# A streaming encoder layer on one core: token-major values first, 24 projection tiles in pairs by seven half products, the other tiles as fillers

## The chip, the cores and the metric

The kernel runs on one core of a Trainium2 chip. TensorE does the matmuls and transposes, VectorE, ScalarE and GpSimd the elementwise work, and SyncE (SP) issues most of the transfers. The metric is the device time of one execution in microseconds; less is better. In the program's names PE is TensorE, DVE is VectorE, ACT is ScalarE and POOL is GpSimd.

## What is computed

One inference step of one layer for 1024 tokens of a new stream and 16 tokens of each of 8 running streams: 1152 tokens, in 9 tiles of 128. In float32, cut to what matters:

```
h = rms_norm(x, norm_g);  z = h @ w_in + b_in       # (1152, 1024) @ (1024, 6664)
mq, mk, mv, mo, mz, mi, mf, aq, ak, av, az, gm, ga = split(z)
q, k = silu(causal_conv(mq, mk))                     # 4 heads of 128
h_m  = sigmoid(mo) * rms_norm(mlstm_chunks(q, k, mv, mi, mf))
q, k = rms_norm per head of 64 of (aq, ak)           # 8 heads of 64
h_a  = softmax(q @ k / 8 + rel_bias) @ av            # band of 512 + own chunk, cache for the running streams
u_m  = (h_m * silu(mz)) @ w_bm;  u_a = (h_a * silu(az)) @ w_ba
y    = x + (sigmoid(gm) * u_m + sigmoid(ga) * u_a) @ w_out
```

The other outputs are the new mLSTM states, the last rows ahead of the convolution, and the new keys and values.

## The kernel before, in words

Matmuls keep float32 accuracy by splitting both operands: a value is `hi`, its rounding to a shorter format, and `lo`, the rest. `split` lets ScalarE make `hi` and another engine (VectorE unless told otherwise) `lo`, and `mm3` gives three matmuls for one product: hi·hi, hi·lo, lo·hi.

```
def mm3(ps, lhs, rhs, first, last):
    mm(ps, lhs[0], rhs[0], start=first, stop=False)
    mm(ps, lhs[0], rhs[1], start=False, stop=False)
    mm(ps, lhs[1], rhs[0], start=False, stop=last)
```

The normed input stays on chip as `h_hi`, `h_lo`: features on partitions (8 k-tiles of 128), tokens along the columns. A projection tile is 128 output features: `load_nt` brings 128 weights x 8 k in two pieces of 512 columns (`wr`, then `wh` and `wl`), `feature_tile` goes over three chunks of 384 tokens with 8 `mm3` each. So a tile is 72 matmuls of 384 columns. The 36 tiles of `wn` are mq, mk, mo and mz (4 each), az (4), gm and ga (8 each). Token-major products have the tokens on the output's partitions: the values mv with the gates i and f (`mv_half`, 264 and 256 columns, weights `w_hi`, `w_lo`), and q, k, v of a pair of attention heads (`qkv`, 384 columns).

The stages are: prenorm of the 9 token tiles, with the first half of the values in between; `gate_rows`, which turns i and f into the decay rows of the mLSTM (ten small transposes `pg`, and a chain of small operations on VectorE and ScalarE between them); convolutions (`conv_part`: first tap on ScalarE, three on VectorE, then tanh and a product) with the projections mq, mk of the same tile; the second half of the values; then per head h the inputs of head h+1, `gate_unit` (mo and mz) and `mlstm_head(h - 1)`. So projections stand beside memory and output chains in this whole part.

In the attention the order of TensorE's work is written by a planner in the kernel: chains `attend(p, i)` (pair p, token tile i: transposes of q and k, scores `pS`, softmax, transposes `pT`, values `pv`) and `sample(p)` are threads that go on when the planner's clock `line.now` says that what they wait for should be there; between them it puts one `mm3` (three matmuls, counted as 480 ns) of `pair_work` (the q, k, v of the next pair), then of `tile_work` (az, gm, ga), then of `um_work` (w_bm). The tile az of the next pair waits until the old pair's tiles are done. At the end stand w_ba and w_out. A tile framework puts the instructions on the engines' queues and adds the semaphores; on each engine they run in that order. SP's list is one such queue: a DMA that waits for its source holds back those behind it.

## Time and profile before

| what | value |
|---|---|
| time, median of 3 runs | 1078.8 us (1077.47 to 1081.25) |
| span of the profiled execution | 1075.1 us |
| TensorE busy, matmuls | 1055.1 us, 98% |
| TensorE busy, weight loads (beside the matmuls) | 1024.3 us |
| VectorE busy | 658.3 us, 61% |
| ScalarE busy | 421.3 us, 39% |
| GpSimd busy | 241.4 us, 22% |
| DMA | 131.58 MB, mean 122 GB/s |

The busy time of a matmul runs until its modelled end, so that neighbours overlap: 0.33 us busy stand behind a start every 0.17 us. What a matmul takes from TensorE is therefore read from the starts in a timeline. A wait is put down to the semaphore that came last.

### The profile page before, as it was taken

To read this page: it belongs to the slowest core of one execution; us is meant where nothing else is said; L and a number is where in the kernel's file an instruction comes from. 1 tells how busy PE (TensorE), PEld (TensorE's weight loads), DVE (VectorE), ACT (ScalarE), POOL (GpSimd) and SP (SyncE) were. 2 spreads that over 40 slices of the span, in tenths; PEclk is the share of its full clock that TensorE was granted. 3 is DMA by queue.
4 is the path that set the end of the run, shared out by engine and by line. 5 is a ranking of instruction groups with operands and counts; after the bars stand their busy time and mean duration, and the time that the engine had idled before them with its cause. 6 is when DMAs were issued, how large, how long until landed. Compare 5 with 4: busy or idle time off the path is not lost.

```text
span 1075.1 us, 19715 instructions
## 1 busy us (share of the span) xinstructions
PE 1055.1 (98%) x7078; PEld 1024.3 (95%) x7078; DVE 658.3 (61%) x1931; ACT 421.3 (39%) x976; POOL 241.4 (22%) x406
## 2 busy tenths in 40 slices
...
PEclk9999999999999999999999999999999999999999
...
GB/s 241 161 88 61 101 66 53 87 121 101 116 85 127 151 146 167 117 76 111 114 126 99 62 148 137 54 71 141 111 79 84 111 262 243 202 223 106 136 143 67
DMA packets 115664, 131.58 MB, mean 122 GB/s; under 512 B 28197, under 2 KB 91885, under 8 KB 115566
## 3 DMA queue, kind: packets, MB, share of 16 engines
...
q14 instruction: 42, 0.34, 0.1%
...
## 4 chain that ended last, share of the span: by engine, by line
PE 88%; DMA 6%; DVE 3%; ACT 1%; issue 1%; SPq 1%; POOL 0%; DVEq 0%; ACTq 0%
PE pm L114 24%; PE pm L116 24%; PE pm L115 24%; PE pT L570 3%; PE pv L732 3%; DMA v_sc<-vt 1%; PE pS L702 1%; PE pS L703 1%; DMA tm<-tg_sc 1%; PE pv L816 1%; DMA xt<-in_x 1%; DMA sm_sc<-tm 1%; DMA raw<-o_sc 1%; PE mA L495 1%; PE mS L477 1%
## 5 line engine op out<-in xcount | busy, mean ns | idle before, releaser
L114 PE MATMUL pm<-h_hi,wh 128*128 128x384 f32 x1056 | 357.4, 339 | 3.2 <-DVE tm L904 3.1
L116 PE MATMUL pm<-h_hi,wl 128*128 128x384 f32 x1056 | 357.5, 339 | 0.0
L115 PE MATMUL pm<-h_lo,wh 128*128 128x384 f32 x1056 | 356.9, 338 | 0.0
L114 PEld LDWEIGHTS pm<-h_hi,wh 128*128 128x128 f32 x1056 | 198.4, 188 | 8.0 <-DVE tm L904 3.2
L116 PEld LDWEIGHTS pm<-h_hi,wl 128*128 128x128 f32 x1056 | 198.3, 188 | 1.3
L115 PEld LDWEIGHTS pm<-h_lo,wh 128*128 128x128 f32 x1056 | 198.4, 188 | 0.6
L114 PE MATMUL pm<-w_hi,h_hi 128*128 128x384 f32 (+2 forms) x432 | 142.6, 331 | 8.2 <-DVE vt L243 5.4
L116 PE MATMUL pm<-w_hi,h_lo 128*128 128x384 f32 (+2 forms) x432 | 140.0, 325 | 1.2 <-DVE h_lo L100 1.2
L115 PE MATMUL pm<-w_lo,h_hi 128*128 128x384 f32 (+2 forms) x432 | 139.9, 325 | 0.0
L99 ACT ACTIVATE wh<-wr 128x512 fp32r<-128x512 f32 x104 | 65.1, 628 | 170.9 <-PE pm L115 131.8
L100 DVE TENSOR_TENSOR wl<-wr,wh 128x512 fp32r<-128x512 f32 x100 | 77.6, 776 | 68.1 <-ACT wh L99 68.0
L114 PEld LDWEIGHTS pm<-w_hi,h_hi 128*128 128x128 f32 x432 | 82.3, 191 | 13.8 <-DVE vt L243 6.0
L562 ACT ACTIVATE prob<-prob,mx 128x640 f32<-128x640 f32 (+4 forms) x72 | 51.2, 711 | 86.4 <-DVE mx L561 66.5
L116 PEld LDWEIGHTS pm<-w_hi,h_lo 128*128 128x128 f32 x432 | 82.4, 191 | 2.7 <-DVE h_lo L100 1.7
L564 POOL TENSOR_SCALAR prob<-prob,mx 128x640 f32<-128x640 f32 (+4 forms) x72 | 50.7, 704 | 150.2 <-DVE mx L563 83.7
L115 PEld LDWEIGHTS pm<-w_lo,h_hi 128*128 128x128 f32 x432 | 82.5, 191 | 0.1
L114 PE MATMUL pm<-x_hi,wh 128*128 128x384 f32 x192 | 65.1, 339 | 0.0
L116 PE MATMUL pm<-x_hi,wl 128*128 128x384 f32 x192 | 65.0, 339 | 0.0
L115 PE MATMUL pm<-x_lo,wh 128*128 128x384 f32 x192 | 65.0, 338 | 0.0
L559 DVE CUSTOM_DVE_ANT_0 prob<-pS,bias 128x640 f32<-128x640 f32 (+4 forms) x64 | 41.8, 654 | 16.6 <-PE pT L570 8.4
L981 POOL TENSOR_TENSOR sa<-sa 128x384 f32<-128x384 f32 x24 | 27.7, 1163 | 107.2 <-DVE sa L980 107.2
L994 DVE SCALAR_TENSOR_TENSOR xr<-pm,xr 128x384 f32<-128x384 f32 x24 | 13.4, 558 | 62.2 <-PE pm L116 62.2
...
## 6 DMA issues: line engine op xcount, KB each, us to landing
wr<-in_wn SPq DMA_DIRECT2D x72, 256.0 KB, 2.9
...
kr<-in_Kc SPq DMA_DIRECT2D x16, 512.0 KB, 5.2
vr<-in_Vc SPq DMA_DIRECT2D x16, 512.0 KB, 5.2
...
xt<-in_x SPq DMA_DIRECT2D x9, 512.0 KB, 5.3
...
```

The lines of the kernel that those rows point to most:

```text
L99: act.activation(out=hi, in_=raw, func=AF.Copy)
L100: eng.tensor_tensor(out=lo, in0=raw, in1=f(hi), op=ALU.subtract)
L114: mm(ps, lhs[0], rhs[0], start=first, stop=False)
L115: mm(ps, lhs[0], rhs[1], start=False, stop=False)
L116: mm(ps, lhs[1], rhs[0], start=False, stop=last)
L559: dve.tensor_tensor_reduce(out=view, in0=pS, in1=bias, scale=1.0, scalar=-3e38, op0=ALU.add, op1=ALU.max, accum_out=mx[:, 0:1])
L562: act.activation(out=pt[:, :nk], in_=pt[:, :nk], func=AF.Exp, bias=mx[:, 1:2], accum_out=mx[:, 2:3])
L564: pool.tensor_scalar(out=pt[:, :nk], in0=pt[:, :nk], scalar1=mx[:, 3:4], scalar2=1.0, op0=ALU.mult, op1=ALU.mult)
L570: pe.transpose(pT[:, n * P:(n + 1) * P], pt[:, n * P:(n + 1) * P], ident)
L732: mm(pv[:, j * 256:(j + 1) * 256], at("Vst")[:, i + 1 - nb + n, j, :], st[:, n].rearrange("p a q -> p (a q)"), start=n == 0, stop=n == nb - 1)
L981: pool.tensor_tensor(out=sm[:, s], in0=sm[:, s], in1=ta[:, s], op=ALU.add)
L994: dve.scalar_tensor_tensor(out=xr, in0=ps.rearrange("p (i t) -> p i t", i=3), scalar=0.5, in1=xr, op0=ALU.mult, op1=ALU.add)
```

## The change

The whole front part of the program is written in another order, and 24 of the 44 projection tiles are computed in another way.

- The prenorm leaves the input in quarters: k-tiles 0 to 3 and 4 to 7 (`h1`, `h2`), tokens 0 to 575 and 576 to 1151 (`h21` is k 0 to 3 of the second half). For tokens of the second half it also makes four sums and differences of quarters, `S1` to `S4`, each split into hi and lo.
- Then all values, mv and av, token-major, in four passes over the nine tiles with four sets of weights; the results go to `v_sc` in DRAM. `h21` is stored to `h_sc`.
- Then 12 pairs of tiles: aq with ak (with the norm of q and k feature-major, by a matmul with a block of ones, `pN`), mq with mk, mo with mz. A pair is a product of a 2 x 2 block of weight halves with a 2 x 2 block of input quarters; it is computed with seven half products instead of eight (`chunk_of`), 4 k-tiles and 288 columns each, twice for the two chunks of a half. The weight sums come from GpSimd (`sub` in `pair_weights`), the sums of results from VectorE and GpSimd. Outputs go to `qk_sc`, `u_sc`, `g_sc` in DRAM.
- Then `h21` is loaded back, `gate_rows`, `head_inputs` (which now reads `u` from DRAM), and the four mLSTM heads, with two tiles of gm behind each. The tiles, now in four chunks of 288 columns, take `lo` of their weights from GpSimd.
- The attention reads q, k and v from DRAM (`load_q`, `load_kv`); the transposes of q and k and `pair_work` are gone; 8 gate tiles, az and w_bm are what the planner can put between the chains, and it counts 520 ns for three such matmuls. The keys leave the kernel feature-major and are transposed on the host.

```diff
+    h1 = [hp.tile([P, KH, HF], F32R, name=f"h1_{q}") for q in ("hi", "lo")]
+    h2 = [hp.tile([P, KH, T], F32R, name=f"h2_{q}") for q in ("hi", "lo")]
...
+        if n1 < P:
+            n, s = P - n1, slice(c0 + n1 - HF, c1 - HF)
+            x21, x22 = (px[:, :, n1:P] for px in pxs)
+            s1, s2 = (x0.tile([P, KH, P], F32, tag="sx", name="sx", bufs=5)[:, :, 0:n] for _ in range(2))
+            act.activation(out=s1, in_=x22, func=AF.Copy)
+            dve.tensor_tensor(out=s1, in0=x21, in1=s1, op=ALU.add)
+            x11, x12 = (x0.tile([P, KH, P], F32, tag="sx", name="sx", bufs=5)[:, :, 0:n] for _ in range(2))
+            pool.tensor_tensor(out=x11, in0=f(h1[0][:, :, s]), in1=f(h1[1][:, :, s]), op=ALU.add)
+            pool.tensor_tensor(out=x12, in0=f(h2[0][:, :, s]), in1=f(h2[1][:, :, s]), op=ALU.add)
+            pool.tensor_tensor(out=s2, in0=s1, in1=x11, op=ALU.subtract)
+            split(S_hi[0][:, :, s], S_lo[0][:, :, s], s1, pool)
+            split(S_hi[1][:, :, s], S_lo[1][:, :, s], s2, pool)
+            s3 = x0.tile([P, KH, P], F32, tag="sx", name="sx", bufs=5)[:, :, 0:n]
+            dve.tensor_tensor(out=s3, in0=x11, in1=x21, op=ALU.subtract)
+            split(S_hi[2][:, :, s], S_lo[2][:, :, s], s3, pool)
+            pool.tensor_tensor(out=s2, in0=x12, in1=s2, op=ALU.subtract)
+            split(S_hi[3][:, :, s], S_lo[3][:, :, s], s2)
...
+    wts = None
+    for i in range(NT):
+        prenorm(i)
+        if i == 0:
+            wts = value_weights(0, pool)
+        values(0, i, wts)
+    for u in range(1, 4):
+        wts = value_weights(u, dve)
+        for i in range(NT):
+            values(u, i, wts)
+    for q in range(2):
+        sp.dma_start(h_sc[q], f(h21[q]))
...
+    def pair_weights(n1, n2):
+        def load(n, q):
+            t_ = wp.tile([P, KH, P], F32, tag="wr", name="wr", bufs=7)
+            sp.dma_start(t_, a["wn"][n][:, KH * q:KH * q + KH, :])
+            return t_
+        def halves(x):
+            hi = wp.tile([P, KH, P], F32R, tag="wh", name="wh", bufs=8)
+            lo = wp.tile([P, KH, P], F32R, tag="wl", name="wl", bufs=8)
+            split(hi, lo, x)
+            return hi, lo
+        def sub(out, x, y):
+            pool.tensor_tensor(out=out, in0=x, in1=y, op=ALU.subtract)
+        b11, b12, b22, b21 = load(n1, 0), load(n2, 0), load(n2, 1), load(n1, 1)
+        w = {1: halves(b11)}
+        sub(b11, b12, b11)
+        w[5] = halves(b11)
+        t2 = wp.tile([P, KH, P], F32, tag="t2", name="t2", bufs=1)
+        sub(t2, b22, b11)
+        w[6] = halves(t2)
+        w[2] = halves(b21)
+        w[3] = halves(b22)
+        sub(b12, b22, b12)
+        w[7] = halves(b12)
+        sub(b21, b21, t2)
+        w[4] = halves(b21)
+        return w
+    def product(ps, w, x, first):
+        for k in range(KH):
+            for l, r in ((0, 0), (0, 1), (1, 0)):
+                mm(ps, w[l][:, k, :], x[r][:, k, :], start=first and k + l + r == 0, stop=k == KH - 1 and l == 1, skip_group_check=True)
...
+    def chunk_of(w, s, ev):
+        X, W, Z = (pp.tile([P, 512], F32, tag=t_, name=t_)[:, :HC] for t_ in ("pX", "pW", "pZ"))
+        p1, p5, u2, t_ = buf(), buf(), buf(), buf()
+        product(X, w[1], quarter(0, 0, s), True)
+        act.activation(out=p1, in_=X, func=AF.Copy)
+        product(W, w[5], sums(1, s), True)
+        act.activation(out=p5, in_=W, func=AF.Copy)
+        pool.tensor_tensor(out=t_, in0=p1, in1=p5, op=ALU.add)
+        product(Z, w[6], sums(2, s), True)
+        add(dve, u2, Z, p1)
+        yield
+        product(X, w[2], quarter(0, 1, s), False)
+        ev(0, 0, s, X, False)
+        product(W, w[3], sums(4, s), False)
+        add(dve, u2, W, u2)
+        ev(1, 0, s, u2, True)
+        product(Z, w[7], sums(3, s), False)
+        add(dve, t_, Z, t_)
+        ev(1, 1, s, t_, True)
+        yield
+        product(Z, w[4], quarter(1, 1, s), False)
+        add(dve, p1, Z, p1)
+        ev(0, 1, s, p1, True)
+        yield
...
+        def ev(e, half, s, x, own):
+            n = 36 + 4 * e + p
+            z, y, t_ = (x if own else buf()), buf(), buf()
+            c, b = (wp.tile([P, HC], F32R, tag=f"sq{q}", name="sq", bufs=2) for q in range(2))
+            act.activation(out=z, in_=x, func=AF.Identity, bias=bn[:, n:n + 1])
+            act.activation(out=y, in_=z, func=AF.Square)
+            split(c, b, y, pool)
+            pn = pp.tile([P, 512], F32, tag="pN", name="pN")[:, :HC]
+            mm(pn, onesb, c, start=True, stop=False)
+            mm(pn, onesb, b, start=False, stop=True)
+            act.activation(out=y, in_=pn, func=AF.Ln, scale=1.0 / 64, bias=eps)
+            act.activation(out=y, in_=y, func=AF.Exp, scale=-0.5)
+            dve.scalar_tensor_tensor(out=t_, in0=y, scalar=-0.5 / 64, in1=y, op0=ALU.mult, op1=ALU.mult)
+            dve.scalar_tensor_tensor(out=t_, in0=pn, scalar=64 * EPS, in1=t_, op0=ALU.add, op1=ALU.mult)
+            dve.scalar_tensor_tensor(out=y, in0=t_, scalar=1.5, in1=y, op0=ALU.add, op1=ALU.mult)
+            dve.scalar_tensor_tensor(out=z, in0=z, scalar=gqk[:, e:e + 1], in1=y, op0=ALU.mult, op1=ALU.mult)
+            c_ = cols(half, s)
+            sp.dma_start(qk_sc[4 * e + p][:, c_], z)
...
+    jobs = [(36 + p, 40 + p, ev_norm(p)) for p in range(4)]
+    jobs += [(h, 4 + h, ev_plain(h, 4 + h)) for h in range(4)]
+    jobs += [(8 + h, 12 + h, ev_gate(h)) for h in range(4)]
+    last = None
+    for n1, n2, ev in jobs:
+        w = pair_weights(n1, n2)
+        for s in range(2):
+            ch = chunk_of(w, s, ev)
+            next(ch)
+            if last:
+                next(last)
+            next(ch)
+            last = ch
+    next(last)
...
+    h21 = [hq.tile([P, KH, HF], F32R, name=f"h21_{q}") for q in ("hi", "lo")]
+    for q in range(2):
+        sp.dma_start(f(h21[q]), h_sc[q])
...
+    def conv_part(nt, out):
...
-        def ev(c, ps):
-            lo, hi = c * CH, min((c + 1) * CH, TP)
-            act.activation(out=u[:, 3 + lo:3 + hi], in_=ps[:, :hi - lo], func=AF.Identity, bias=bn[:, nt:nt + 1])
-            if hi == TP:
...
-        feature_tile(w, h_rhs, ev)
+        sp.dma_start(u[:, 3:3 + TP], u_sc[nt][:, 0:TP])
+        sp.dma_start(us[:, :, 3:], u_sc[nt][:, TP:T].rearrange("p (b t) -> p b t", b=NB))
...
-    mv_half(0)
     gate_rows()
     prev = head_inputs(0)
-    mv_half(1)
...
-    gate_unit(0)
-    for h in range(1, 4):
-        cur = head_inputs(h)
-        gate_unit(h)
-        mlstm_head(h - 1, *prev)
-        prev = cur
-    mlstm_head(3, *prev)
-    for j in range(3):
-        feature_tile(load_nt(a["wn"][20 + j]), h_rhs, g_evac(j))
+    for h in range(4):
+        nxt = head_inputs(h + 1) if h < 3 else None
+        mlstm_head(h, *prev)
+        prev = nxt
+        for _ in range(2):
+            j = gates.pop(0)
+            feature_tile(load_nt(a["wn"][20 + j], eng=pool), h_rhs, g_evac(j), n=HC)
...
     def attend(p, i):
-        while (p, i) not in made:
+        while p and ("s", p - 1, NPT - 1) not in done:
             yield
-        zt, zd, t_ = made[p, i]
-        yield from until(t_)
+        if i == 0:
+            load_bias(p)
+            load_q(p, 1)
...
-        sX.give(t_)
-        sZ.give(t_)
...
         done.add(("s", p, i))
+        if i == 3 and p < 3:
+            load_q(p + 1, 0)
+            load_kv(p + 1)
...
         while p < 4 or gates:
             if p < 4 and (not p or all((p - 1, i) in done for i in range(6))):
-                w = load_nt(a["wn"][16 + p])
-                ev = silu_evac(16 + p, lambda c: at("za")[:, c * CH:(c + 1) * CH])
-                for c in range(NCH):
+                w = load_nt(a["wn"][16 + p], eng=pool)
+                ev = silu_evac(16 + p, lambda c: za[:, c * HC:(c + 1) * HC])
+                for c in range(4):
...
     def um_work():
...
-            w = load_nt(a["wbm"][j], 4)
-            for c in range(NCH):
+            w = load_nt(a["wbm"][j], 4, eng=pool)
+            for c in range(4):
                 yield from chunk(c, w, h_rhs, um_evac(j), 4)
```

The instructions on TensorE where `gate_rows` starts, in the program before (L114 to L116 are the three matmuls of `mm3`, `pg` the transposes of `gate_rows`):

```order
L115 MATMUL pm<-h_lo,wh 128x384
L254 MATMUL pg<-ident,gscr 36x128
L255 MATMUL pg<-ident,gscr 36x128
L116 MATMUL pm<-h_hi,wl 128x384
...
L114 MATMUL pm<-h_hi,wh 128x384
L274 MATMUL pg<-ident,gscr 1x36
...
L275 MATMUL pg<-ident,gscr 1x36
L116 MATMUL pm<-h_hi,wl 128x384
...
L291 MATMUL pg<-ident,gscr 32x1
L292 MATMUL pg<-ident,gscr 32x1
L116 MATMUL pm<-h_hi,wl 128x384
```

The same place after the change, between the last half product (L322) and the first tile of gm (L123 to L125):

```order
L322 MATMUL pZ<-h_lo,wh 128x288
L322 MATMUL pZ<-h_hi,wl 128x288
L505 MATMUL pg<-ident,G 36x128
L506 MATMUL pg<-ident,G 36x128
L525 MATMUL pg<-ident,gscr 1x36
L526 MATMUL pg<-ident,gscr 1x36
L542 MATMUL pg<-ident,gscr 32x1
L543 MATMUL pg<-ident,gscr 32x1
L573 MATMUL pg<-ident,gscr 128x36 x4
L123 MATMUL pm<-h_hi,wh 128x288
```

Before, 35, 4 and 24 projection matmuls stand between the groups of transposes shown; after, all ten transposes stand in one block with none between.

SP's list at that place after the change (`g_sc<-ring` stores of the last pairs, `u` the input of a convolution, `wr` the weights of the first tile of gm):

```order
L411 DMA g_sc<-ring 128x288
L513 DMA gscr<-in_m 4x8
L592 DMA u<-in_convst 128x8x3
L593 DMA u<-u_sc 128x1024
L594 DMA u<-u_sc 128x8x16
L411 DMA g_sc<-ring 128x288
...
L434 DMA h_hi<-h_sc 128x2304
L434 DMA h_lo<-h_sc 128x2304
...
L570 DMA M_sc<-gscr 36x128
L445 DMA wr<-in_wn 128x512
```

Before, a weight load was ahead of the store of the decay rows there:

```order
L284 DMA out_mp<-gscr 1x4
L106 DMA wr<-in_wn 128x512
L290 DMA dec_sc<-gscr 1x32
...
L305 DMA DEC<-dec_sc 128x64
L106 DMA wr<-in_wn 128x512
L319 DMA M_sc<-gscr 36x128
L420 DMA Mb<-M_sc 128x9x128
```

What moved: `u` is a transfer now and not written by ScalarE, it is issued after a store of the last pair, and the first weights of gm come behind the store of the decay rows.

TensorE where a pair takes over from the one ahead of it in the attention, before (`pX` transposes of q and k, `pS` scores, `pv` values, `pT` transposes of the probabilities):

```order
L115 MATMUL pm<-w_lo,h_hi 128x384
L702 MATMUL pS<-Kst,q_hi 128x128
L703 MATMUL pS<-Kst,q_lo 128x128
L579 MATMUL pX<-ident,zd 128x128 x2
L116 MATMUL pm<-w_hi,h_lo 128x384
L114 MATMUL pm<-w_hi,h_hi 128x384
L732 MATMUL pv<-PT,Vst 128x256 x5
L570 MATMUL pT<-ident,prob 128x128 x5
L115 MATMUL pm<-w_lo,h_hi 128x384
```

And at a pair's turn after the change (`pv<-vr` and `px` are of the running streams):

```order
L999 MATMUL px<-sel,R 128x64 x2
...
L778 MATMUL pT<-ident,prob 128x128 x5
L911 MATMUL pv<-PT,Vst 128x256 x5
L879 MATMUL pS<-Kst,q_hi 128x128
L880 MATMUL pS<-Kst,q_lo 128x128
L911 MATMUL pv<-PT,Vst 128x256 x5
L778 MATMUL pT<-ident,prob 128x128 x5
...
L960 MATMUL pS<-qk 128x128
L962 MATMUL pS<-kr,QB 32x512 x4
L123 MATMUL pm<-h_hi,wh 128x288
```

Before, projections of the next pair stand between the steps of the chains there; after, scores, transposes and values follow each other until the tile az of the next pair may start.

## Rows read from the trace of the kernel before

**Rows 1.** The page: busy times of TensorE, and the granted clock in 40 slices.
```profile
PE 1055.1 (98%) x7078; PEld 1024.3 (95%) x7078; DVE 658.3 (61%) x1931; ACT 421.3 (39%) x976; POOL 241.4 (22%) x406
...
PEclk9999999999999999999999999999999999999999
```

**Rows 2.** Groups of matmuls by shape (count | busy us, mean ns | idle before).
```profile
L114 PE MATMUL pm<-h_hi,wh 128*128 128x384 f32 x1056 | 357.4, 339 | 3.2 <-DVE tm L904 3.1
L114 PE MATMUL pm<-w_hi,h_hi 128*128 128x384 f32 x288 | 99.5, 345 | 0.3 <-DVE zt L605 0.3
L114 PE MATMUL pm<-w_hi,h_hi 128*128 128x264 f32 x72 | 21.6, 304 | 1.7 <-ACT h_hi L99 0.9 <-DVE gscr L247 0.4 <-DVE st L85 0.4
L114 PE MATMUL pm<-w_hi,h_hi 128*128 128x256 f32 x72 | 21.5, 299 | 6.2 <-DVE vt L243 5.4 <-ACT u L370 0.8
L579 PE MATMUL pX<-ident,zd 128*128 128x128 f32 x72 | 13.8, 273 | 0.0
```

**Rows 3.** Timeline of TensorE, 60 to 62 us (start, duration, instruction).
```profile
60.01 0.33 PE L115 MATMUL pm<-h_lo,wh 128*128 128x384 f32 x1
...
61.92 0.34 PE L114 MATMUL pm<-h_hi,wh 128*128 128x384 f32 x1
```

**Rows 4.** Timeline of TensorE, 100 to 103 us.
```profile
101.54 0.28 PE L116 MATMUL pm<-w_hi,h_lo 128*128 128x256 f32 x1
...
102.98 0.28 PE L116 MATMUL pm<-w_hi,h_lo 128*128 128x256 f32 x1
```

**Rows 5.** Waits of TensorE (total us, times, longest).
```profile
PE pm L114 <- DVE vt L243: 5.4, 3, 3.4
```

**Rows 6.** Windows around the value tiles (stretch: length, busy by engine, granted clock).
```profile
97.50:101.40 3.90, 3.85 (x20) 3.86 (x21) 1.59 (x2) 0.00 (x0) 0.00 (x0) 0.57 0.24 67
```

**Rows 7.** Groups by shape on VectorE, ScalarE and GpSimd.
```profile
L382 DVE SCALAR_TENSOR_TENSOR kT<-u,cw,kT 128x1024 f32<-128x1024 f32 x12 | 15.4, 1279 | 2.3 <-ACT kT L380 2.3
L382 DVE SCALAR_TENSOR_TENSOR kT<-u,cw,kT 128x128 f32<-128x128 f32 x12 | 4.7, 393 | 0.0
L243 DVE TENSOR_TENSOR vt<-pm,bv 128x256 f32<-128x256 f32 x18 | 7.6, 422 | 17.3 <-PE pm L116 12.5 <-DMA v_sc<-vt 4.8
L100 DVE TENSOR_TENSOR wl<-wr,wh 128x512 fp32r<-128x512 f32 x100 | 77.6, 776 | 68.1 <-ACT wh L99 68.0
...
L99 ACT ACTIVATE wh<-wr 128x512 fp32r<-128x512 f32 x104 | 65.1, 628 | 170.9 <-PE pm L115 131.8 <-DMA sm_sc<-tm 13.5 <-PE pm L116 7.5
L384 ACT ACTIVATE sg<-kT 128x1152 f32<-128x1152 f32 x4 | 4.7, 1169 | 11.2 <-DVE kT L382 11.2
L99 ACT ACTIVATE w_hi<-wqr 128x264 fp32r<-128x264 f32 x8 | 2.9, 410 | 0.0
L384 ACT ACT_TABLE_LOAD x1 | 1.3, 1283 | 4.6 <-DMA M_sc<-gscr 4.6
...
L100 POOL TENSOR_TENSOR wl<-wr,wh 128x512 fp32r<-128x512 f32 x4 | 5.1, 1292 | 9.4 <-DMA v_sc<-vt 8.6 <-ACT wh L99 0.9
```

**Rows 8.** DMA issues (count, KB each, median us from issue to landing).
```profile
wr<-in_wn SPq DMA_DIRECT2D x72, 256.0 KB, 2.9
...
kr<-in_Kc SPq DMA_DIRECT2D x16, 512.0 KB, 5.2
```

**Rows 9.** Timeline of SP's queue, 84 to 90 us (start, duration of an issue).
```profile
86.49 0.50 SPq L106 DMA_DIRECT2D wr<-in_wn  x1
```

**Rows 10.** Groups by shape: the softmax of one tile.
```profile
L559 DVE CUSTOM_DVE_ANT_0 prob<-pS,bias 128x640 f32<-128x640 f32 x32 | 26.3, 821 | 9.7 <-PE pT L570 8.4 <-PE pS L703 1.0
L563 DVE RECIPROCAL mx<-mx 128x1 f32<-128x1 f32 x72 | 11.5, 160 | 24.9 <-ACT prob L562 24.2
...
L562 ACT ACTIVATE prob<-prob,mx 128x640 f32<-128x640 f32 x40 | 33.2, 830 | 54.0 <-DVE mx L561 37.7 <-DVE st L86 12.0 <-POOL ot L742 2.4
...
L564 POOL TENSOR_SCALAR prob<-prob,mx 128x640 f32<-128x640 f32 x40 | 33.5, 837 | 100.2 <-DVE mx L563 54.3 <-DVE st L85 10.9 <-PE pm L116 6.2
```

**Rows 11.** Windows in the mLSTM stage (columns as in rows 6).
```profile
210.00:220.00 10.00, 10.00 (x59) 9.59 (x58) 9.66 (x26) 4.58 (x10) 4.09 (x5) 1.00 0.51 96
```

596 lines of the change are left out of this document (304 added, 292 removed).

## The prediction

> **What bounds the kernel now.** I began with the busy times and the granted clock of the whole span [rows 1]: TensorE is busy 98% of 1075.1 us and its clock stands in the top tenth in all 40 slices, while VectorE has 61%, ScalarE 39% and GpSimd 22%. A change can thus win by taking columns from TensorE, and loses wherever it makes TensorE wait. Next I read the groups of matmuls [rows 2], because busy time of pipelined matmuls says little: the 384-column ones of the projections are 1056 x 3 (eight-k tiles, um and wba), 288 x 3 (q, k, v of the attention) and those of w_out, which stay. What one of them really costs is the distance between starts in an undisturbed stretch of the timeline: 11 gaps between 60.01 and 61.92 us are 173.6 ns each at 384 columns [rows 3], 12 gaps between 101.54 and 102.98 are 120.0 ns each at 256 [rows 4]. The line through both (0.419 ns a column, 12.8 ns fixed) gives 123.4 ns at 264 and 133.4 ns at 288, the change's width. Last I asked where TensorE does wait: only one wait is long, for `vt` of the value tiles, 5.4 us in 3 times [rows 5], and behind it the granted clock is 0.57 over 3.9 us, which loses another 1.7 [rows 6].
>
> **The change, part by part.** Sums are made against the profiled execution, 1075.1 us; the median of the runs shown, 1078.8, lies 3.7 above it, and I add that at the end.
>
> 1, matmuls. Before: 3744 of 384 columns that the change touches (16 mLSTM tiles 1152, q/k/v 864, 20 gate and z tiles 1440, um 288) are 649.9 us, and 216 + 216 values of 264 and 256 are 52.6: together 702.5. After: values 216 x 0.1234 + 648 x 0.120 = 104.4; the pairs 12 x 2 chunks x 7 products x 12 = 2016, the norm's 64, the tiles 1920, um 384, in all 4384 x 0.1334 = 584.8: together 689.2. That is -13.3. Seven of eight products alone would give more, but every remaining tile also goes from three streams of 384 to four of 288 and pays its fixed part once more. The 72 transposes of q and k [rows 2] go; at 128 columns the line gives 66 ns, -4.8. Together **-18.1**. The 288 gap lies between those of 256 and 384 and the line is short: 2 ns either way are 9 us.
>
> The Trainium skill (TensorE: Matmul & The Clock Gate, Back-to-back issue gap) gives an isolated gap of columns / 2.4 plus 2.5 ns, an estimate of 162.5 ns at 384 and 122.5 at 288. This trace does not agree (173.6). By the page's rule the first term would be -24.2 instead of -13.3 and the end sum 11 lower; the row decides.
>
> 2, the old value wait. The second half of the values ran against the convolutions on VectorE; now values run first and alone. That removes 5.4 + 1.7 = **-7.1** [rows 5, 6]. The four weight sets of the new stage must change three times through eleven buffers; the split of a set (ScalarE 0.41, VectorE 0.42 a piece, by its row of 256 columns [rows 7]) keeps up with eight k-steps of 0.36, the 2.9 us load [rows 8] of the last pieces just fails to: **+3** (0 to 5.4 [rows 5]).
>
> 3, the sums. Each of tiles 5 to 8 gives GpSimd seven 512-column operations at 1.292 us [rows 7], 9.0 us, tile 4 half; 41 us that end long before the pairs start, so values hide them. But ScalarE and the PSUM buffers of the prenorm wait for them in order, and TensorE's transposes behind: **+5** (0 to 15, a third of the 41).
>
> 4, seam from values to pairs. SP's list has the pair weights behind the last value store. After the last matmul: bias 0.42 [rows 7], four or five issues of about 0.5 [rows 9], landing 2.9 [rows 8], ScalarE split 0.63, then the first product, 6.3 in all; and a wait longer than that of [rows 5] again costs 1.7 of clock. **+8** (5 to 10).
>
> 5, the pairs. A plain or gate pair is 22.4 us of TensorE and half of that elsewhere. The four norm pairs have 24.5 on TensorE; on ScalarE 7 splits of 0.628 and 44 operations of 288 columns, 0.43 between its rows, 23.3; on VectorE 7 of 0.776 and 40 of about 0.47, 24.2 [rows 7]. Three engines level: 0 if the chains of different chunks overlap fully, 5 us a pair if they queue. The chains are independent, so nearer the first: **+5** (0 to 20).
>
> 6, seam from pairs to mLSTM, the largest term. In the old TensorE order projections stand between the transposes of the gate rows; in the new one all ten stand in one block, with the first filler behind them. From the last product: add, tanh and gate product about 1.6; SP then issues the store and head 0's `u`, 3.0; half a megabyte lands in 5.2 [rows 8], 8.2; VectorE's order puts the taps of q and k ahead of the gate rows' last operations: from 8.7, 6 x 1.279 + 6 x 0.393 = 10.0, and about ten small ones at 0.16 to 0.4 [rows 7, 10], 20.8; exponentials and four transposes, 21.5. The filler's weight load stands in SP's list behind the store of `M_sc`, and its split behind a tanh of 1152 columns on ScalarE (1.169) and 1.292 on GpSimd, 24.5. TensorE has nothing else to do. With the clock's 1.7, **+26**; 11 if `u` is there early and the taps are out of the way, 32 if the second half of the weights comes late too. What is late next is head 0's memory chain, which the fillers then cover.
>
> The Trainium skill (ScalarE: Activation LUTs, What ACT_TABLE_LOAD costs) counts a drain of about 1.4 us with each table switch. The change adds two switches in this seam (Ln after Tanh and back); the trace has 1.283 for the load [rows 7] and hides it under `u`'s landing; no run here shows the drain. By the page the seam would be up to 2.8 longer and the end 1121.
>
> 7, mLSTM. In the densest stretch before, VectorE worked 9.66 of 10 us and TensorE lost nothing [rows 11]. Now 745 fillers (99 us) stand where more than twice as many stood, with three heads' convolutions against them: **+5** (0 to 20).
>
> 8, attention. The planner counts 520 ns for three filler matmuls that take 400, so chains get less time than planned. A softmax is 0.821 + 0.830 + 0.837 and two of one column at 0.160, 2.8 us [rows 10], and some 0.9 of handing over; between scores and transposes stand 9 + 23 fillers and more, over 4 us: hidden. At a pair's turn, though, z waits for the old pair's tiles, the projections of the next pair that filled this before are gone, and there is a row of scores, transposes and values alone. There two chains follow one another (2 x 3.7), with splits of 0.63 and more [rows 7] and the last values, some 13 us for 10 of matmuls. Four such places: **+13** (4 to 35).
>
> Sum: -18.1 - 7.1 + 3 + 5 + 8 + 5 + 26 + 5 + 13 = +39.8, 1114.9 us; with the 3.7, **1118.6**.
>
> **Rivals.** The first ends on the other side: *VectorE is never late*. If `u` lands while the last product runs, the taps leave the gate chain and the seam is its bare 11; an engine that has room there has it inside the stages too (terms 3, 5, 7 and the weight changes zero, attention 4, the first seam 5). Then -25.2 + 20 = -5.2, 1073.6. For it speaks that VectorE has 39% free; against it that `u` is issued behind the last pair's stores. It decides when the plus terms stay under 25. The second is *seams only*: the order in SP and TensorE holds, inside the stages nothing waits: -25.2 + 34 = +8.8, 1087.6. The third is *the other engines bind*: norm pairs, mLSTM and the pair turns at their upper ends and the sums at 15: -25.2 + 3 + 15 + 8 + 20 + 26 + 20 + 35 = +101.8, 1180.6. That the saving itself is not there is a fourth: at a gap of 147 ns for 288 (one eighth more than the line) the pairs would bring nothing and term 1 would be +41; [rows 3, 4] leave no room for it.
>
> **How the numbers follow.** Forecast 0.46, seams only 0.16, the other engines bind 0.13, VectorE never late 0.20, and 0.05 for the strip around no change that lies between them; 0.3% (3.2 us) is about what a measurement of this kernel can tell from no change. The range 1072 to 1160 leaves out about half of the first rival and half of the third. The likeliest case alone is 1095 to 1140. Faster 0.20, same 0.05, slower 0.75.
>
> **What would show it.** In the profile after: 288-column matmuls 133 ns apart in the pairs; TensorE busy clearly under 98%; a hole of over 20 us with `pg` transposes alone in it where pairs end, ended by a weight split, and one of 6 to 7 us where values end, both with a lower clock behind; the longest waits in the pages of TensorE being for `wh`/`wl` and small gate operations, not `vt`. I am wrong if the hole at the gate rows is under 12 us, if the attention has no stretch without fillers in which TensorE idles, or if matmuls of 288 are much nearer to 120 ns.

## The result, and the profile after

The changed kernel takes **1230.5 us**, the median of four runs (1223.4 to 1236.3), against 1079.5 for the one before in the same comparison (1077.5 to 1081.3): a ratio of **1.1395** [1.1341, 1.1449]. It is slower, as forecast, and far outside the range. One run of e1 below, at 3741 us against 1188.5 for the other, was disturbed and is left out of all numbers.

The page of the profiled execution after, its first rows and four rows of the 40 slices, each of 30.5 us:

```profile
span 1221.5 us, 22147 instructions
...
PE 1075.7 (88%) x8078; PEld 1028.9 (84%) x8078; DVE 642.4 (53%) x1523; ACT 518.5 (42%) x1100; POOL 426.2 (35%) x509
...
PE   7899798878999992377699999879889899999998
...
PEclk9989999888999996688899999979989899999999
DMA  6424332212322106985754445444362456675442
```

TensorE, 98% busy before [rows 1], has 88%, and its clock has dips where it had none. Counted from 0, the slices show four places: 6 to 9 (the norm pairs), 15 to 16 (pairs to mLSTM, the seam), 17 to 19 (mLSTM) and 25 to 31 (attention). No other engine comes near 100%, and VectorE works less than before, so no engine's total explains the time. The longest waits of TensorE (total us, times, longest):

```profile
PE pm L123 <- ACT tg L466: 18.4, 4, 7.4
PE pm L123 <- ACT wh L119: 18.3, 2, 18.1
PE pN L375 <- DVE ring L380: 17.7, 5, 6.7
PE pS L879 <- DVE mx L767: 9.5, 14, 1.4
...
PE pX L322 <- ACT wh L119: 6.2, 1, 6.2
```

The first is new and was not forecast: `tg` is the tanh that empties the gate tiles' PSUM in the mLSTM. The second is the seam, the third the norm pairs, the fourth the scores of the attention, the last the seam from values to pairs, 6.2 us where 6.3 were worked out.

To put a price on each stage I take for every matmul the time to the next one's start, less the median of that shape in the same trace; what is over is **lost** time. Half-clock matmuls count as lost too. Sums in us, worked out from the records of the two traces:

| | before | after | difference |
|---|---|---|---|
| matmuls at their usual distance | 1011.4 | 983.8 | -27.6 |
| lost: prenorm and values | 23.5 | 35.9 | +12.4 |
| lost: pairs | | 39.1 | +39.1 |
| lost: seam, pairs to mLSTM | | 35.4 | +35.4 |
| lost: mLSTM (before: with gate rows and convolutions) | 6.9 | 50.6 | +43.7 |
| lost: attention, to its last values | 24.2 | 70.9 | +46.7 |
| lost: the rest | 5.7 | 2.4 | -3.3 |

Together +146.4, the difference of the spans. The saving is there, and larger than forecast. (The medians of rare shapes carry waits of their own; with one distance for each shape in both traces the first row is about -25, and the time lost in addition 171 instead of 174.) Matmuls of 288 columns start 133 ns apart, as the line of [rows 3, 4] gave (12 gaps from 159.89 to 161.48):

```profile
159.89 0.30 PE L322 MATMUL pX<-h_hi,wl 128*128 128x288 f32 x1
...
161.48 0.29 PE L322 MATMUL pW<-S_hi,wl 128*128 128x288 f32 x1
```

Of the 174 us lost in addition, 32 are matmuls at about twice their usual distance (492 of them, 48.6 us; before 172, 16.6; short waits may hide among them). Behind the seam's hole the 288-column starts are 240 ns apart, the lower of the two clock levels (granted clock 0.50 from 501 to 505.8 us), until about 506.

### The profile page after: what moved, and what is told of

Its sections match the earlier page's. It is cut to its first block, busy times and chain, and to the rows that moved or that the text cites. A ratio compares the mean times of both kernels' runs of the same rounds, so it can differ in the third digit from the quotient of the medians.

```text
span 1221.5 us, 22147 instructions
## 1 busy us (share of the span) xinstructions
PE 1075.7 (88%) x8078; PEld 1028.9 (84%) x8078; DVE 642.4 (53%) x1523; ACT 518.5 (42%) x1100; POOL 426.2 (35%) x509
## 5 line engine op out<-in xcount | busy, mean ns | idle before, releaser
L123 PE MATMUL pm<-h_hi,wh 128*128 128x288 f32 (+1 forms) x864 | 269.3, 312 | 40.0 <-ACT tg L466 18.4
L124 PE MATMUL pm<-h_lo,wh 128*128 128x288 f32 (+1 forms) x864 | 268.4, 311 | 0.0
L125 PE MATMUL pm<-h_hi,wl 128*128 128x288 f32 (+1 forms) x864 | 266.4, 310 | 1.3 <-POOL wl L120 1.3
L123 PEld LDWEIGHTS pm<-h_hi,wh 128*128 128x128 f32 x864 | 169.0, 196 | 46.6 <-ACT tg L466 20.3
L119 ACT ACTIVATE wh<-wr 128x512 fp32r<-128x512 f32 (+2 forms) x176 | 102.1, 589 | 182.7 <-PE pm L124 90.7
L125 PEld LDWEIGHTS pm<-h_hi,wl 128*128 128x128 f32 x864 | 167.9, 195 | 3.0 <-POOL wl L120 1.8
L120 DVE TENSOR_TENSOR wl<-wr,wh 128x512 fp32r<-128x512 f32 (+1 forms) x120 | 91.7, 772 | 57.9 <-ACT wh L119 55.3
L120 POOL TENSOR_TENSOR wl<-wr,wh 128x512 fp32r<-128x512 f32 (+1 forms) x56 | 70.9, 1271 | 66.2 <-ACT wh L119 63.5
L123 PE MATMUL pm<-wh,h_hi 128*128 128x256 f32 (+1 forms) x272 | 79.7, 295 | 4.8 <-ACT h_hi L119 2.3
L124 PE MATMUL pm<-wl,h_hi 128*128 128x256 f32 (+1 forms) x272 | 78.6, 290 | 2.7 <-DVE wl L120 2.2
L125 PE MATMUL pm<-wh,h_lo 128*128 128x256 f32 (+1 forms) x272 | 78.4, 290 | 0.3 <-DVE h_lo L120 0.2
L325 DVE TENSOR_TENSOR ring<-pZ,ring 128x288 f32<-128x288 f32 x72 | 32.7, 455 | 65.3 <-PE pZ L322 53.4
L123 PE MATMUL pm<-x_hi,wh 128*128 128x384 f32 x192 | 64.6, 337 | 1.2 <-ACT x_hi L119 1.2
L322 PE MATMUL pX<-h_hi,wh 128*128 128x288 f32 x192 | 58.6, 305 | 7.9 <-ACT wh L119 6.2
L125 PE MATMUL pm<-x_hi,wl 128*128 128x384 f32 x192 | 64.5, 336 | 0.0
L322 PE MATMUL pW<-S_hi,wh 128*128 128x288 f32 x192 | 59.0, 307 | 3.9 <-ACT ring L334 3.9
```

Of the source, the lines that this page charges most:

```text
L119: act.activation(out=hi, in_=raw, func=AF.Copy)
L120: eng.tensor_tensor(out=lo, in0=raw, in1=f(hi), op=ALU.subtract)
L322: mm(ps, w[l][:, k, :], x[r][:, k, :], start=first and k + l + r == 0, stop=k == KH - 1 and l == 1, skip_group_check=True)
L325: eng.tensor_tensor(out=out, in0=x, in1=y, op=ALU.add)
```

## The experiments

Each ratio is to the kernel before on the same chip, with its 95% interval. First a look at a norm pair, since TensorE is at 93 of 120 us there (all engines, 206 to 219 us; start, duration, instruction, idle before it):

```profile
207.66 1.28 POOL L301 TENSOR_TENSOR t<-wr 128x512 f32<-128x512 f32 x1
208.29 1.20 DVE L120 TENSOR_TENSOR wl<-wr,wh 128x512 fp32r<-128x512 f32 x1 [3.38 <-ACT wh L119]
208.90 1.72 POOL L301 TENSOR_TENSOR wr<-wr 128x512 f32<-128x512 f32 x1
209.91 1.25 DVE L120 TENSOR_TENSOR wl<-t,wh 128x512 fp32r<-128x512 f32 x1 [0.42 <-ACT wh L119]
211.09 1.27 DVE L120 TENSOR_TENSOR wl<-wr,wh 128x512 fp32r<-128x512 f32 x1
212.28 2.48 DVE L379 SCALAR_TENSOR_TENSOR ring<-ring 128x288 f32<-128x288 f32 x2
214.68 0.81 DVE L380 SCALAR_TENSOR_TENSOR ring<-pN,ring 128x288 f32<-128x288 f32 x2
215.27 0.58 PE L375 MATMUL pN<-sq,onesb 128*128 128x288 f32 x1 [6.74 <-DVE ring L380]
```

The two buffers `pN` are freed by L380, and ahead of it on VectorE stand three `wl`, weight splits for a pair *further on*. TensorE's matmul of the next norm waits for a buffer, and on TensorE the half products stand behind it. Counted over the whole stretch: from the second norm pair on, 10 or 11 splits of later pairs stand on VectorE ahead of the first L380 of a norm pair.

**e1, the order of the pairs.** One norm pair, one plain pair, and so on, instead of four norm pairs in a row.

```diff
-    jobs = [(36 + p, 40 + p, ev_norm(p)) for p in range(4)]
-    jobs += [(h, 4 + h, ev_plain(h, 4 + h)) for h in range(4)]
+    jobs = []
+    for p in range(4):
+        jobs += [(36 + p, 40 + p, ev_norm(p)), (p, 4 + p, ev_plain(p, 4 + p))]
```

> The four norm pairs alternate with the four plain pairs instead of standing in a row; nothing else changes. In the changed kernel's trace TensorE loses 36.6 us between 200 and 320 us, where the norm pairs stand, and nothing in the plain and gate pairs. If it is the average load (ScalarE, VectorE and GpSimd full for four pairs on end), half idle pairs in between take up the rest: that loss falls under 12 us and the time by about 25 us, to 1205. If it is the chain inside a pair (two pN buffers that come free only behind the next pair's weight splits), it goes with each norm pair wherever it stands: the loss stays over 28 us and the time within 8 us of 1230.

1188.5 us in one run, ratio 1.10: 42 less than the median of the changed kernel, whose four runs lie 13 us apart, and 35 less from profile to profile. The pairs lose 5.5 instead of 39.1, every other stage is within 3 of what it was, but for the end (w_out), which loses 5 more. Windows of the pairs after (start:end, length, busy PE, PEld, DVE, ACT, POOL, clock, DMA share, GB/s), then of e1:

```profile
205.00:325.00 120.00, 93.19 (x628) 90.07 (x627) 76.65 (x146) 68.43 (x158) 49.98 (x47) 0.89 0.25 79
325.00:465.00 140.00, 139.38 (x1052) 139.15 (x1051) 63.59 (x123) 66.78 (x131) 39.70 (x42) 1.00 0.22 69
```

```profile
149.00:290.00 141.00, 139.18 (x1024) 138.29 (x1025) 105.91 (x182) 91.08 (x207) 69.03 (x62) 0.98 0.32 105
```

By the signs set down ahead of the run, a loss under 12 us speaks for the load of four norm pairs on end, and against a wait that goes with each norm pair. The load alone does not explain it: in e1 VectorE works 106 of 141 us, 75%, and TensorE loses almost nothing, while after it had 77 of 120, 64%, and TensorE lost a fifth. A norm pair is about 27 us of VectorE for 24.5 of TensorE, some 9 us too much in four. What did change besides is the order in VectorE's queue: in e1 a single split of a later pair stands ahead of the first L380 of the second, third and fourth norm pair, where there were 10 or 11. That this order is the cause is read from the traces; e1 changes it and the mix of pairs at once, and no run changes the order alone.

**e2, the attention's loads held back** until the third head is stored (`with tc.issue_after(stored[2, 2].ins): run_line()`). **e3, whole rows for the convolutions:** `u` comes in one transfer a row, the running streams' part and the state are copied to their places on chip by GpSimd. **e4, gate tiles rationed,** two a pair, with az and the gates in generators of their own and five buffers for `wh` and `wl` instead of three.

```diff
-        sp.dma_start(us[:, :, 0:3], a["convst"][nt])
-        sp.dma_start(u[:, 3:3 + TP], u_sc[nt][:, 0:TP])
-        sp.dma_start(us[:, :, 3:], u_sc[nt][:, TP:T].rearrange("p (b t) -> p b t", b=NB))
+        sp.dma_start(c0, a["convst"][nt])
+        sp.dma_start(u[:, 3:3 + T], u_sc[nt])
+        pool.tensor_copy(out=us[:, :, 0:3], in_=c0)
+        pool.tensor_copy(out=us[:, :, 3:], in_=u[:, 3 + TP:].rearrange("p (b t) -> p b t", b=NB))
```

> The attention's loads and all else that it puts on SP are issued only behind the last store of the third mLSTM head. In the changed kernel the mLSTM stage (501 to 695 us) loses 50 us while the DMA engines are 0.7 to 1.0 busy, and the first attention operands are loaded in it. If these loads crowd out the stage's own, the loss falls by 10 to 20 us. If the stage's own transfers (inputs of the convolutions, broadcast rows, weights) fill the queues by themselves, the loss changes by less than 5 us, and the time stays at 1230 or rises by up to 8 because the attention starts with late operands.

> The convolutions' inputs of the running streams are loaded as whole rows and spread by GpSimd, their last rows gathered by GpSimd and stored as rows of 96 bytes: 3 x 1024 packets of 12 and 64 bytes per input become 3 x 128. Between 465 and 625 us 25600 packets of 12 and 64 bytes take 315 of 1839 us of DMA engine time, 20 us of each engine. If the queues' busy time is what makes operands late, seam and mLSTM together (83 us lost) lose 10 to 20 us less, and the time is 1210 to 1220. If it is the order of issues on SP or the large transfers, they lose less than 5 us less.

> In the attention the gate tiles get a generator of their own, so that they can be placed while az waits for the old pair, and two of them are kept for each pair; there are five weight buffers in place of three. In the changed kernel the attention (698 to 1025 us) loses 70 us, 50 of them at the three turns of a pair, where TensorE has no tile to put between the chains. If missing fillers are the cause, that loss falls to 25 to 40 us and the time to 1190 to 1200. If the chains are late for another reason (an engine or the transfers), the loss moves between the stretches and the total stays within 10 us of 1230.

| run | us | ratio | lost: pairs | seam | mLSTM | attention |
|---|---|---|---|---|---|---|
| after | 1230.5 | 1.1395 | 39.1 | 35.4 | 50.6 | 70.9 |
| e2 | 1226.7 | 1.1378 [1.1253, 1.1502] | 41.4 | 34.8 | 49.6 | 72.2 |
| e3 | 1196.7 | 1.1099 [1.1056, 1.1143] | 37.7 | 27.9 | 28.5 | 71.1 |
| e4 | 1239.3 | 1.1495 [1.1423, 1.1566] | 39.3 | 34.1 | 53.6 | 77.5 |

Neither the loads of the attention (e2) nor a ration of gate tiles (e4) makes a difference for the better. e3 takes 22 from the mLSTM and 7.5 from the seam, more than the 10 to 20 that were expected; its end loses 5 more, so that its profile is 26 shorter. The wait in the mLSTM after (all engines, 505 to 524 us):

```profile
510.07 0.61 SPq L445 DMA_DIRECT2D wr<-in_wn  x1
...
519.89 0.63 ACT L119 ACTIVATE wh<-wr 128x512 fp32r<-128x512 f32 x1 [9.21 <-DMA wr<-in_wn]
520.43 0.48 ACT L466 ACTIVATE tg<-pm,bh 128x288 f32<-128x288 f32 x1
...
520.97 0.61 PE L123 MATMUL pm<-h_hi,wh 128*128 128x288 f32 x1 [7.37 <-ACT tg L466]
```

A quarter megabyte issued at 510.07 lands 9.8 us later; 2.9 was the median [rows 8]. ScalarE waits for it at the head of its queue, and behind it stands the tanh that would empty a PSUM buffer whose product is done. So TensorE waits, by name, for a tanh, and in truth for a DMA. The transfers of this stretch, after (465 to 625 us) and then in e3 (463 to 625 us): packets, bytes, the queue's share of 16 engines, and the stores of `tg` (KB each, us to landing):

```profile
DMA packets 44149, 24.46 MB, mean 153 GB/s; under 512 B 27975, under 2 KB 39915, under 8 KB 43883
...
q1 hardware_dynamic: 44139, 24.34, 73.8%
...
tg_sc<-tg SPq DMA_DIRECT2D x17, 144.0 KB, 7.9
```

```profile
DMA packets 26484, 29.74 MB, mean 184 GB/s; under 512 B 5671, under 2 KB 21693, under 8 KB 26216
...
q1 hardware_dynamic: 26472, 29.59, 62.0%
...
tg_sc<-tg SPq DMA_DIRECT2D x23, 144.0 KB, 2.9
```

More bytes in the same time, and the stores land in 2.9 instead of 7.9. The 25,600 packets of 12 and 64 bytes, nearly all of which e3 takes away, occupied 315 of the 1890 us that the queue's packets took in that stretch, 20 us of each of 16 engines; seam and mLSTM together lose 29.6 less. The edit also makes two loads of three for each input; the two were not taken apart. The Trainium skill (DMA: Bandwidth & Descriptors, Specifications) wants 512 bytes or more in a transfer for line rate; e3 agrees with it in direction.

**e5, the gate rows earlier:** `gate_rows()` is called between the fourth and the fifth pair, its scratch beside the weights. **e6, the planner's latency factor** 2.3 to 1.5. **e7** is e1, e3 and gate rows ahead of the eighth pair; **e8** is e7 with 1.5. In e5, e7 and e8 the ring has 17 buffers instead of 20, so that some gate products are taken from buffers already written again: these results are not the right ones, the work is the same.

> The gate rows are computed ahead of the first plain pair, on the PSUM buffers of the norm; their scratch takes three of the 20 buffers of the ring. In the changed kernel the seam between pairs and mLSTM loses 35.4 us. If the chain of the gate rows, behind the taps of the convolutions, holds it, what is left is the first filler's weights after the last product and the reload of h21, and the seam loses 12 us or less: the time is about 1207. If the transfers there (2.4 MB of h21, two convolution inputs, C, v) hold the weights anyway, it loses 20 to 30 us and the time is 1217 to 1225.

> One number of the attention's planner changes: the factor on its estimated latencies, 2.3 before, is 1.5. The stage loses 70.9 us, nearly all where less than 4 of 12.5 us are fillers, and a ration of the gate tiles did not help. If the planner puts too many fillers between the steps of a chain (7.7 us between the scores and the transposes of 640 keys, which need about 3.7) and has none left for the rest, fewer per step last longer: the stage loses 35 to 55 us and the time falls by 15 to 35 us. If the chains are really that slow, TensorE comes to each step too early, waits, and the loss stays within 8 us or grows.

> Three edits together: norm and plain pairs alternate, rows of the running streams are loaded whole, the gate rows are computed ahead of the last plain pair. Alone the first took 34 us from the loss of the pairs and the second 30 us from seam and mLSTM. If the causes are independent and the third leaves 12 us in the seam, the time is 1230 - 34 - 30 - 16 = 1150. If the third gives nothing, 1166. If what one gives the other takes (the same queues), over 1175.

> The three edits and the planner's factor 1.5. If the factor's gain is of the attention alone, it adds here what it gives alone, 15 to 35 us, and the time is 1115 to 1135. If the chains are as slow as planned, it is that of the three edits alone, within 8 us.

| run | us | ratio | lost: pairs and seam | mLSTM | attention |
|---|---|---|---|---|---|
| e5 | 1225.8 | 1.1390 [1.1357, 1.1423] | 72.7 | 49.3 | 73.1 |
| e6 | 1254.6 | 1.1658 [1.1610, 1.1707] | 73.8 | 50.2 | 85.4, and 20.9 behind it |
| e7 | 1163.1 | 1.0808 [1.0771, 1.0845] | 45.1 | 21.6 | 68.4 |
| e8 | 1189.2 | 1.1050 [1.1018, 1.1082] | 43.5 | 21.8 | 81.1, and 16.3 behind it |

e5 is a miss: with the gate rows out of the seam the hole stays, 18.0 and 14.7 us at the next two things that wait, the convolution of the first key and the memory. The gate rows were the first of three chains of nearly the same length. In e7 one hole of 23.7 is left there, and its pairs lose about 20 where they lose 5.5 in e1: its gate rows stand among them, with three buffers fewer (e9 below, with 20, loses 9 there). A smaller latency factor makes chains come back too early and TensorE wait for them: 25 us worse twice.

**e12 is e1 and e3 together. e9 adds** the gate rows early (20 buffers again, one less for loaded weights) and one gate tile ahead of the first head's memory. **e13 is e9** with that tile's weights issued ahead of the reload of `h21`:

```diff
-    for q in range(2):
-        sp.dma_start(f(h21[q]), h_sc[q])
...
     gates = list(range(16))
+    ahead = [load_nt(a["wn"][20], eng=pool)]
+    for q in range(2):
+        sp.dma_start(f(h21[q]), h_sc[q])
```

> The alternating pairs and the whole rows of the running streams together, without the early gate rows: the ground for the next two. If the two gains add, 1230 - 42 - 33 = 1155; with part of the waits shared, 1160 to 1170.

> To the two edits come the gate rows ahead of the last plain pair (their scratch now reuses its own buffers, and one of seven weight loads' buffers goes) and one tile of gm ahead of the first mLSTM head. In the run with early gate rows TensorE stood 23.7 us behind the last product, for the convolution of the first key. With a tile that needs only weights and h21 in front, it should start 6 to 10 us after the last product and cover 13 us of that chain: 10 to 18 us less than the two edits alone. If the transfers of h21 and of the convolutions hold the tile's weights, it saves under 6.

> As the run with the early gate rows and a first tile ahead of the first head, but that tile's weights are loaded ahead of h21 and not behind it. There TensorE started 22.7 us after the last product, on weights issued 0.4 us behind the 2.4 MB of h21 and landing 11 us later. If these transfers hold the seam, the weights land 3 to 5 us after issue, TensorE starts 10 to 14 us after the last product, and the time falls by 8 to 14 us, to 1141 to 1147. If the engines' order (taps and tanh ahead of the weight split) holds it, TensorE starts after 18 us or more and the time changes by less than 5 us.

| run | us | ratio | lost: pairs and seam | mLSTM | attention |
|---|---|---|---|---|---|
| e12 | 1155.9 | 1.0730 [1.0699, 1.0761] | 32.9 | 26.0 | 71.4 |
| e9 | 1155.0 | 1.0722 [1.0663, 1.0780] | 31.5 | 20.8 | 72.8 |
| e13 | 1145.2 | 1.0639 [1.0608, 1.0670] | 25.3 | 26.6 | 66.5 |

e1 and e3 add up: 1230.5 - 42.0 - 33.8 = 1154.7 against 1155.9; by the profiles' spans 1221.5 - 35.0 - 26.2 = 1160.3 against 1155.2. e9 is a miss, 0.9 instead of 10 to 18: its first tile starts 22.7 us behind the last product. The seam of e9 and of e13 (all engines, rows of the first gate tile's weights and product):

```profile
442.41 0.33 SPq L528 DMA_DIRECT2D h_hi<-h_sc  x1
...
445.06 2.77 SPq L539 DMA_DIRECT2D wr<-in_wn  x2
...
457.09 0.61 PE L123 MATMUL pm<-h_hi,wh 128*128 128x288 f32 x1 [22.55 <-ACT wh L119]
```

```profile
442.69 0.82 SPq L536 DMA_DIRECT2D wr<-in_wn  x2
443.56 1.12 SPq L574 DMA_DIRECT2D h_hi<-h_sc  x1
...
450.88 0.61 PE L123 MATMUL pm<-h_hi,wh 128*128 128x288 f32 x1 [16.64 <-ACT wh L119]
```

The weights behind 2.4 MB of `h21` land some 11 us after their issue, ahead of it 7.5: the hole falls from 22.6 to 16.6 and the time by 9.8. The time is what was expected, the steps are not: the weights were to land in 3 to 5 us and TensorE to start after 10 to 14. Of the 11.9 between the profiles 6.2 are seam; the mLSTM loses 5.8 more, the attention 6.3 less and the end about 5 less, none of which was followed. So the place in the queue is worth about 6 us here, and the rest is luck.

**What binds the attention.** On e12 the number of gate tiles that stay for the attention is set: **e11** puts four behind each head and leaves none, **e10** none and leaves 16 (`for _ in range(4)` and `range(0)`). **e14** is e12 with three live chains and a third buffer each for `prob` and `PT`. **e15** is e13 with 400 ns counted for three fillers instead of 520, **e16** e10 with 400. **e17** is e10 with the gates in a generator of their own, so that they never wait for az. **e18** is e13 with the gates in a generator of their own that hands out 1/24 of their fillers for each `attend` that is done.

> On the ground of the two edits all 16 gate tiles stand in the mLSTM stage, four for each head, none in the attention: 102 us of matmuls move out of the attention. If TensorE bounds the attention, that stage gets 100 us shorter and the time stays within 10 us of the two edits alone. If its chains of scores, softmax, transposes and values bound it (about 350 us for 32 tiles and 4 samples whatever stands between), it gets less than 45 us shorter, and the time rises by 50 us or more.

> The other way: all 16 gate tiles stand in the attention, none in the mLSTM stage, 102 us more of matmuls there. If TensorE bounds both stages, the time stays within 10 us of the two edits alone. If the attention is bound by its chains, its 70 us of loss take up a good half of them and the stage grows by 45 to 70 us; the mLSTM stage gets as much shorter as its own chains let it: by 90 us if they never bind (then the time falls by 20 to 40), by 40 or less if they do (then the time rises).

> On the ground of the two edits (1155.9) three tiles of the attention may be under way instead of two, with three buffers each for the probabilities and their transposes; scores and transposes keep their one PSUM tile each. The stage takes 359 us with 287 us of matmuls, and 324 us with 222 us of them. If too few chains in flight set that floor, the stage gets 20 us shorter or more. If the single PSUM tiles for scores and transposes, or the in-order engines, set it, it changes by less than 8 us.

> On the best version so far (1145.2): the attention's planner counts three filler matmuls as 400, what they take at 133 ns each, instead of 520. A step that it places so many ns behind another then has 1.3 times as many fillers in front of it. If the steps come too early in real time because the fillers are overcounted, the stage (347 us, 66 of loss) loses 20 to 40 us less; the fillers end sooner, so not all of the loss goes: 1105 to 1130. If the single PSUM tiles or the engines set the pace, more fillers per step only push the last steps into a stretch without any, and the time stays within 8 us or rises.

> The same number on the run with all 16 gate tiles in the attention (1242.3), where fillers are never short: 95 us of them were left over behind the last values while the stage lost 63 us. If the spacing is the cause, that loss falls under 35 us and the time by 25 to 40 us. If PSUM tiles or engines set the pace, the loss stays over 50 us and the time within 10 us.

> All 16 gate tiles in the attention again, and a generator of their own for them without any ration, so that a tile is to be had at every point of the chains, also while az waits for the old pair; five weight buffers. In the runs before, a third to a half of the loss stood in stretches of 12.5 us with less than 4 us of fillers, and with 16 tiles 95 us of fillers were still left at the end, because az stood in front of them. If missing cover at those places is the cause, the stage's loss falls from 63 to 25 to 35 us (the kernel before loses 24 with fillers everywhere), and the time by 25 to 40 us from 1242. If the chains are late by themselves, it stays over 50.

> On the best version (1145.2) the eight gate tiles of the attention are spread evenly over the chains of the first three pairs, a matmul group at a time, in a generator of their own. Together az, the gates and w_bm are 195 us of cover for 92 us of chain work, where the kernel before had over 320. If the loss depends on the cover that each stretch has (0.5 to 0.8 us lost in 12.5 with over 7.5 us of fillers, 2 to 2.5 with 4 to 7.5, over 6 with less than 4), even cover loses 45 to 58 us instead of 66: 1124 to 1137. If the turns of a pair themselves lose it, it stays within 6 us.

| run | us | ratio | attention: length | its matmuls | lost | from there to w_out |
|---|---|---|---|---|---|---|
| after | 1230.5 | 1.1395 | 358.2 | 287.4 | 70.9 | 59.6 |
| e12 | 1155.9 | 1.0730 | 358.8 | 287.4 | 71.4 | 59.6 |
| e13 | 1145.2 | 1.0639 | 347.5 | 281.0 | 66.5 | 59.6 |
| e11 | 1199.4 | 1.1134 [1.1053, 1.1215] | 324.1 | 221.7 | 102.4 | 55.5 |
| e10 | 1242.3 | 1.1532 [1.1459, 1.1606] | 348.2 | 285.5 | 62.7 | 166.0 |
| e14 | 1207.6 | 1.1219 [1.1130, 1.1307] | 315.7 | 207 | 108 | 151.1 |
| e15 | 1158.0 | 1.0716 [1.0684, 1.0748] | 360.5 | 290.6 | 69.9 | 54.2 |
| e16 | 1243.8 | 1.1498 [1.1467, 1.1529] | 370.3 | 305.9 | 64.4 | 146.5 |
| e17 | 1242.5 | 1.1529 [1.1481, 1.1578] | 352.6 | 285.8 | 66.8 | 166.7 |
| e18 | 1165.1 | 1.0809 [1.0767, 1.0852] | 354.9 | 276.8 | 78.1 | 63.2 |

Against e12, with 66 us less of matmuls (e11) the stage is only 35 shorter and loses a third of itself; with eight more tiles to draw from (e10) it draws no more of them than before, and they run alone at the end, while the mLSTM, with none, loses 93.8. So TensorE alone does not set the length of this stage; for a good part the chains do, as the planner spaces them. Windows of a pair with fillers and of one with few, after, then the stretch of e11 that idles most, then, for the same part of the program, one of the kernel before:

```profile
698.00:787.00 89.00, 87.17 (x776) 81.10 (x775) 36.15 (x104) 47.45 (x101) 43.93 (x59) 1.00 0.49 156
787.00:877.00 90.00, 78.40 (x662) 69.03 (x662) 39.60 (x121) 44.01 (x94) 38.42 (x58) 0.92 0.43 140
```

```profile
868.00:949.00 81.00, 61.94 (x559) 51.02 (x563) 43.23 (x134) 44.99 (x94) 39.40 (x64) 0.84 0.45 142
```

```profile
687.00:787.00 100.00, 100.00 (x770) 96.31 (x769) 73.80 (x263) 48.68 (x124) 37.53 (x70) 1.00 0.31 100
```

No engine is full where TensorE idles: VectorE 44 and 53%, ScalarE 49 and 56%, and in a stretch without any filler (961 to 973 us) 55 and 53%, GpSimd 57%; the kernel before had VectorE at 74% and TensorE full. What is left is the latency of the steps. A pair's turn after (TensorE, 790 to 799 us):

```profile
792.65 0.86 PE L911 MATMUL pv<-PT,Vst 128*128 128x256 f32 x5 [0.65 <-DVE PT L120]
794.18 0.77 PE L778 MATMUL pT<-ident,prob 128*128 128x128 f32 x5 [0.67 <-POOL prob L772]
795.44 0.33 PE L879 MATMUL pS<-Kst,q_hi 128*128 128x128 f32 x1 [0.49 <-DVE mx L767]
...
796.92 1.30 PE L778 MATMUL pT<-ident,prob 128*128 128x128 f32 x5 [1.04 <-DVE PT L120]
```

Each step waits for another engine, with no filler between. In bins of 12.5 us, 5 bins with under 4 us of fillers lose 34 us, 12 bins with 4 to 7.5 lose 31, the 12 with more lose 6; before, 32 of 36 bins had more than 7.5. But no experiment mends it. A third chain (e14) shortens the stage by 43 us, as it should if too few chains are in flight, but with 80 us less of matmuls in it, which then stand at the end, and the time rises by 52. A free supply (e17) leaves the turns as bare as before. A shorter count changes nothing with 16 tiles (e16) and costs 13 us with eight (e15); an even spread (e18) costs 20.

**No version beats the kernel before;** the best is e13, 6.4% above it.

## Why the prediction was wrong

The sum was +39.8, measured are +146.4 of span. Three steps failed, each a wait taken too low: the norm pairs (34.1 too little), the mLSTM (38.7) and the attention (33.7), together 106.5 of the 106.6 missing. The other terms were off as well, by +9.4, +3.5, -9.5 and -3.3, and it is luck that these cancel. By its own steps:

1. *Matmuls, -18.1:* measured -27.6, right in kind. The 288 gap was 133.0 where 133.4 was said; 2.4 more come from the 384-column ones (174.2 each), 1.7 from the 288, and the transposes taken out were worth 107.6 ns each, not the 66 of the line (3.0 more); the last 2.4 come from the medians of rare shapes.
2. to 4. *Value wait, sums, first seam, +8.9 together:* measured +12.4, and the hole between values and pairs 6.2 for 6.3.
5. *Norm pairs, +5:* measured 39.1. The step that failed is "the chains are independent, so nearer the first". It weighed the engines' loads, which came out near (VectorE about 27 us a pair for 24.2), and left out that VectorE's queue holds the weight splits of later pairs ahead of the operation that frees `pN`. In e1, where one split stands there instead of 10 or 11, 34 of the 39 go; that the order does it, and not the lighter pairs between, is read from the traces.
6. *Seam, +26:* measured 35.4; the place, the order in SP's list and the wait for `wh` are as forecast, the size is 9 off. The gate rows were done earlier than said (last transposes at 482.3, some 17 behind the last product instead of 21.5), the first product of the filler far later, at 35.8 instead of 24.5. In between stands SP's list (all engines, 490 to 502 us):

```profile
493.60 0.34 SPq L570 DMA_DIRECT2D M_sc<-gscr  x1
496.41 0.34 SPq L445 DMA_DIRECT2D wr<-in_wn  x1
...
499.24 1.16 ACT L603 ACTIVATE sg<-qT 128x1152 f32<-128x1152 f32 x1 [16.75 <-DMA M_sc<-gscr]
...
500.31 0.61 ACT L119 ACTIVATE wh<-wr 128x512 fp32r<-128x512 f32 x1
...
500.97 0.61 PE L123 MATMUL pm<-h_hi,wh 128*128 128x288 f32 x1 [18.10 <-ACT wh L119]
```

   The gate rows' last operation on ScalarE ends at 482.5, but the store of `M_sc` is issued 11 us later, behind other transfers that wait in turn, the longest for `out_convs`, a store in packets of 12 bytes. The tanh, which takes over the gate rows' buffer, waits for that store, and the weight split stands behind the tanh. The sum counted nothing for the wait in SP's list. Transfers are what e3 and e13 change: e3 takes 7.5, e13 some 6 by moving the weights ahead of `h21`. The two table switches take 1.28 us each with the next operation right behind.
7. *mLSTM, +5:* measured +43.7. The step that failed looked at VectorE alone [rows 11] (and counted 745 fillers where eight tiles are 768). The queue of transfers, in the kernel before, in the stretch of its mLSTM and convolutions (120 to 380 us):

```profile
DMA packets 31360, 25.68 MB, mean 99 GB/s; under 512 B 12903, under 2 KB 26091, under 8 KB 31339
...
q1 hardware_dynamic: 31339, 25.41, 39.7%
```

   It went from 39.7 to 73.8%, with twice the small packets in three fifths of the time. Half of the loss goes with e3; the other half, 20.8 to 28.5 in e3, e7 to e9, e12 and e13, was not taken apart.
8. *Attention, +13:* measured +46.7. The mechanism was right in kind, turns without fillers. The step that failed is the sum of four turns of 3.25: the barest five bins, at the turns, lose 34, and the other half lies between the turns, where fillers are thin and where the step took all waits to be hidden. With q, k and v went 150 us of matmuls (864 by the gap of [rows 3]), nearly all of which had stood beside the chains. By e10, e11 and e17 the chains, as the planner spaces them, and not the supply of fillers set this stage's length. Why the planner still puts scores, transposes and values of several chains in a row at the turns when tiles are free **stays open**; a latency factor above 2.3, which the misses of e6 and e8 point to, was not tried.

The misses add up: 34.1 for the pairs, 9.4 seam, 38.7 mLSTM, 33.7 attention, 3.5 ahead of them, less 9.5 and 3.3: 106.6. The nearest rival, *the other engines bind* at 1180.6, named the right stages, but its upper ends of 20, 20 and 35 were exceeded in all three, and no engine was full: what the traces show in its place is an order in a queue, a DMA queue and latencies.
